# The first 40 microseconds of a decoder step: a weight copy moved to VectorE, the first matmuls sorted by kind, and the sums of squares in four wide batches

## The chip, the core and the metric

The kernel runs on one core of one Trainium2 chip. The metric is device microseconds from the start to the end of one execution. Three executions of the kernel before took 1449.05, 1449.08 and 1451.44 us, the median is 1449.08 us.

In what follows PE is TensorE (matmuls), PEld its weight loads, DVE is VectorE, ACT is ScalarE, POOL is GpSimd, and SP is the engine whose queue issues nearly all loads of weights.

## The reference

One inference step of a one-layer decoder, for a prompt of 256 tokens and 8 sample tokens, with a model width of 2048. All arithmetic is float32.

```python
xn = rmsnorm(x, g_mix)
z = xn @ w_in                                  # 2048 x 5128: inputs of two head groups
xr, conv_new = causal_conv(z[..., OFF_RGX:OFF_RGG], conv_buf, conv_w, conv_b)
...                                            # RG-LRU group and mLSTM group
x = x + jnp.concatenate([y_rg, y_ml], axis=-1) @ w_out
xq = (rmsnorm(x, g_xa) @ w_xa_q).reshape(B, L, XA_HEADS, XA_DH)
...                                            # attention over 256 memory tokens
x = x + o @ w_xa_o
xf = rmsnorm(x, g_ffn)
x = x + (jax.nn.silu(xf @ w_ffn_gate) * (xf @ w_ffn_up)) @ w_ffn_down
```

`rmsnorm` is `x * rsqrt(mean(x * x) + 1e-6) * g`. The change touches the first two lines alone: the norm of the input and the beginning of the product with `w_in`.

## The kernel before, in words

**Layout.** Activations stand with the features on the 128 partitions and the 264 tokens (256 + 8) along the free axis, as 16 chunks of 128 features each. `xres` holds the input that way. A product is a sequence of steps (the list `steps`). Most steps make 128 output features from all 16 input chunks and accumulate in one PSUM bank.

**Splitting.** A float32 product is made from parts in the type fp32r. Each operand is split in a high part and a low part: ACT copies the operand to fp32r (high), and DVE subtracts that copy from the operand (low). `mm3` then issues three matmuls: high weights times high input, high weights times low input, low weights times high input. In the words below these are hh, hl and lh. The weights of a step come in two halves of 1024 columns (512 KB each, tile `raw`, five buffers). ACT and DVE write the high and the low part of a half in one tile `w` (four buffers). A buffer of `raw` is free for SP's next load when both have read it.

**The norm comes late.** The factor `rsqrt(mean(x*x))` depends on the token alone, so products use the input times the gain (`g_mix`), and the results are multiplied by the factor when they leave PSUM. The sum of squares over features is built in `acc_x` (128 x 264): ACT squares, DVE adds. Matmuls with a vector of ones (`token_sums`) then add over partitions, DVE takes the inverse square root, and `spread` puts it back along the tokens in `rstd`.

**The first four steps** are special. They make four output blocks at once, in four PSUM banks `first`, and take four input chunks per step, so that PE can begin when a sixteenth of the input and of these weights has landed. One such sixteenth is called a chunk here, 0 to 15: an input piece (132 KB) and a weight piece (128 x 512, 256 KB), of which `split_first` makes high and low parts, and 12 matmuls (four banks times hh, hl, lh). Steps 4 to 6 are ordinary steps; step 7 has the gates.

**What sets the order.** Code is written as one program; a scheduler may reorder instructions of PE, DVE and ACT within their dependences, except inside a manual schedule, where the written order holds. SP's order is always as written. In the kernel before, PE's order is manual from step 4 to step 6 only. The squares are in two parts: eight of 128 x 264 after the splits of step 2 (seven of them with an addition on DVE), and two of 128 x 1056 with four additions after the splits of step 4. In step 5, before its chunk 9, PE issues `token_sums` of `acc_x`; in step 6, before its chunk 8, it issues `spread`. Both places are fixed in the program.

**Warm-up.** Before data has landed, PE runs eight float32 matmuls on a tile of ones that DVE sets.

Of the kernel before, what the change touches and what calls it, by code (L numbers as in the profile page):

```python
# [10 lines left out]
F32 = mybir.dt.float32  # L11
F32R = mybir.dt.float32r
I32 = mybir.dt.int32
AF = mybir.ActivationFunctionType
# [3 lines left out]
P = 128  # L18
# [4 lines left out]
N = T + NS  # L23
# [72 lines left out]
def layer_kernel(ctx: ExitStack, tc, xT, memT, vec, wrg, w_in, w_out, w_q, w_k, w_v, w_o,  # L96
                 w_gu, w_d0, w_d1, w_d2, c0T, kcT, vcT,
                 o_y, o_h, o_cp, o_cs, o_pc, o_sc, o_sn, o_m, o_k, o_v):
    nc = tc.nc
    act, dve, pe = Engine(nc.scalar, price_act), Engine(nc.vector, price_dve), Engine(nc.tensor, price_pe)  # L100
# [8 lines left out]
    def in_order():  # L109
        return tc.manual_schedule(engines={mybir.EngineType.Activation, mybir.EngineType.DVE})  # L110
# [4 lines left out]
    def nm(s):  # L115
        uid[0] += 1
        return f"{s}_{uid[0]}"

    def B(shape, dt=F32):
        return sb.tile(shape, dt, tag="B", bufs=NB, name=nm("B"))  # L120
# [12 lines left out]
    BW = 4 * N + 32  # L133
# [83 lines left out]
    def split_first(i, h):  # L217

        wh, wl = wrows(sb.tile([P, WW], F32R, tag="w", bufs=4, name=nm("w")), i)
        r = raws[i][h].rearrange("p (c m) -> p c m", m=P)  # L220
        with tc.high_priority(), in_order():
            for c in range(2):
                x, k = 4 * i + 2 * h + c, slice(4 * c, 4 * c + 4)
                split(*xn(x), xres[:, x, :], V("g_mix", x))
                st["split"] = act.activation(wh[:, k], r[:, k], AF.Copy)
                dve.tensor_sub(wl[:, k], r[:, k], wh[:, k].bitcast(F32))
        splits[i, h] = (wh, wl)

    def last_squares():

        a, b = (B([P, BW])[:, 0: 4 * N] for _ in range(2))
        for t, q in ((a, 2), (b, 3)):
            act.activation(t, xres[:, 4 * q: 4 * q + 4, :].rearrange("p c n -> p (c n)"), AF.Square)
        dve.tensor_add(a, a, b)
        dve.tensor_add(a[:, 0: 2 * N], a[:, 0: 2 * N], a[:, 2 * N:])
        dve.tensor_add(a[:, 0: N], a[:, 0: N], a[:, N: 2 * N])
        dve.tensor_add(acc_x, acc_x, a[:, 0: N])

    def wrows(w, i):

        w = w[:, WO: WO + 8 * N].rearrange("p (c n) -> p c n", n=N)
        return w[:, :, 0: P], w[:, :, P: 2 * P]
# [14 lines left out]
    def by2(x):  # L257

        return x.rearrange("p (a b) -> p a b", b=2)

    def turn(x):

        return x.rearrange("p (b a) -> p a b", b=2)
# [9 lines left out]
    def mm3(ps, a, b, start, stop):  # L273
        ah, al = a
        bh, bl = b
        ps, bh, bl = by2(ps), turn(bh), turn(bl)
        pe.matmul(ps, ah, bh, start=start, stop=False)
        pe.matmul(ps, ah, bl, start=False, stop=False)
        pe.matmul(ps, al, bh, start=False, stop=stop)

    st = {}
# [49 lines left out]
    ones = const.tile([P, P], F32, name="ones")  # L331
# [6 lines left out]
    def warm(n, w=None):  # L338

        ps = bank()  # L340
        for _ in range(n):
            pe.matmul(ps[:, :P], ones if w is None else w.to_broadcast([P, P]), ones, start=True, stop=True)

    warm(8)
    onesr = const.tile([P, P], F32R, name="onesr")
    mask = const.tile([P, P], F32, name="mask")
    pool_e.affine_select(out=mask, in_=ones, pattern=[[1, P]], compare_op=OP.is_ge, fill=0.0,
# [3 lines left out]
    def V(name, j=0, w=1):  # L351
        o = _V[name][0] + j
        return vecs[:, o: o + w]
# [67 lines left out]
    def sumsq(acc, x, first):  # L421
        if first:
            return act.activation(acc, x, AF.Square)
        s = tmp(x.shape[-1])
        i = act.activation(s, x, AF.Square)
        dve.tensor_add(acc, acc, s)
        return i

    def split(h, l, x, g):

        act.activation(h, x, AF.Copy, scale=g)
        dve.scalar_tensor_tensor(l, x, g, h.bitcast(F32), op0=OP.mult, op1=OP.subtract)
# [27 lines left out]
    xres = const.tile([P, KC, N], F32, name="xres")  # L460
    acc_x = const.tile([P, N], F32, name="acc_x")
# [531 lines left out]
    rx = lambda c: st["xn"](c)  # L993

    first = [bank("ax"), bank("ax"), bank("ax"), bank()]

    def pe_first(q):
        def f(i):
            w = W(i)
            for c in range(4):  # L1000
                for n in range(4):
                    mm3(first[n][:, :N], w(4 * c + n), rx(4 * q + c), q + c == 0, q + c == 6)
        return f

    def evac_first(_):
# [35 lines left out]
    def norm_x():  # L1041
        yield from rstd_from(acc_x, rstd, D)
# [388 lines left out]
    def load_x(e, lo, hi):  # L1431
        e.dma_start(xres[:, lo:hi, :], xT[:, lo:hi, :])
# [24 lines left out]
    for i, (src, cols, pef, evf, need) in enumerate(steps):  # L1457
        if i > 1:
            load_piece(i + LD - 1)
        if i == 7:  # L1460
            st["rg"] = side(rg_gen(), 0)
        if "pend" in need:
            with tc.high_priority(300):
                for e, x in pend:
                    e(x)
            pend = []
        for q in need:
            if q in st:
                finish(lambda: st[q].done)
        if not 4 <= i < 7:  # L1470
            with tc.high_priority(300):
                for e, x in pend:
                    e(x)
            pend = []
        if i == len(steps) - 1:
            kept.enter_context(tc.manual_schedule(engines={mybir.EngineType.PE}))
        now = pe.clock
        dve.clock, act.clock = max(dve.clock, now), max(act.clock, now)
        split_half(i + LS, 0)
        if i + LS < len(steps) and steps[i + LS][1] > 1024:  # L1480
            split_half(i + LS, 1)
        if i == 4:
            kept.enter_context(tc.manual_schedule(engines={mybir.EngineType.PE}))
        ps = pef(i)
        if i == 6:
            kept.close()
        if i == 1:
            with tc.issue_after(st["split"].ins):
                for c in range(8):
                    sumsq(acc_x, xres[:, c, :], c == 0)  # L1490
        if i == 3:
            with tc.issue_after(st["split"].ins), tc.high_priority():
                last_squares()
            st["rstd_x"] = Gen(norm_x())
        if evf is not None:
            pend.append((evf, ps))
        if i == 0:
            for c in range(0, 4, 2):
                load_x(sp, 12 + c, 14 + c)
                load_first(3, c)  # L1500
                load_first(3, c + 1)
        else:
            load_piece(i + LD)
        pump(pe.clock + SLACK)
        if i == 24:
            st["ng"] = side(ml_norm(), 6)
        if i == 57:
            PACE["full"] = False
        if i == 44:
            pool_e.dma_start(kept_k, ml["kb"])  # L1510
            for q in range(2):
                pool_e.dma_start(kept_v[q], ml["vts"][q])
        if i == 40:
            st["memg"] = side(mem_gen(), 7)
# [3 lines left out]
    for lo, hi in ((0, 1), (1, 2), (2, 4), (4, 6), (6, 8), (8, 10), (10, 12), (12, 14), (14, 16)):  # L1518
        for c in range(lo, hi):
            e, r = (pool_e, rstd) if c in POOLC else (dve, fin["ps"][:, :N])  # L1520
# [111 lines left out]
```

## Time and profile before

| | |
|---|---|
| median of three executions | 1449.08 us |
| the profiled execution | 1449.35 us |
| its span (first to last instruction) | 1447.4 us |
| PE busy | 1432.6 us, 99% of the span |
| DVE busy | 1046.6 us, 72% |
| ACT busy | 793.9 us, 55% |
| idle time of PE that a wait explains, over the span | 7.4 us in 12 waits |

The profile's page gives busy times and groups; the timeline gives the instructions in order, each row with its start, its length, the engine, the line, the operation, the tiles and, in brackets, the idle time of the engine before it with what ended it. Nearly all instructions carry the line of a recording helper (L61), so tiles are what tells them apart: `w<-raw` is the splitting of weights, `B<-xres,vecs` the splitting of the input, `t<-xres`, `acc_x` and `B<-xres` belong to the squares, `mm` and `ax` are PSUM banks. Matmuls are pipelined: a row's length includes the drain, so the pace is read from starts.

### The profile page before, as it was taken

The page shows a single profiled execution, that of the slowest core. Times are in us where ns is not written, and L with a number is a line of the kernel's source. Part 1 is how long each engine was busy: PE and PEld are TensorE (multiplying, and loading weights), DVE is VectorE, ACT ScalarE, POOL GpSimd, SP SyncE. Part 2 cuts the span into 40 slices and gives each one's busy share as a digit, 9 for nine tenths or more (in the row PEclk, how much of TensorE's full clock was granted, in tenths as well). Part 3 has the DMA queues.
Part 4 walks back from the last instruction along what each step waited for, and adds up shares of the span by engine and source line. Part 5 has one row for each costly group of instructions (what it writes and reads, how often), then busy time and mean ns, then how long its engine had stood idle before and what let it go on. Part 6 is the DMA issues. An engine that isn't in the chain of part 4 may idle for free.

```text
span 1447.4 us, 29983 instructions
## 1 busy us (share of the span) xinstructions
PE 1432.6 (99%) x11987; PEld 1407.3 (97%) x11987; DVE 1046.6 (72%) x2007; ACT 793.9 (55%) x1286; POOL 127.8 (9%) x203
## 2 busy tenths in 40 slices
PE   9999999999999999999999999999999999999997
PEld 9999999999999999899999999999999999999997
DVE  7966798998899999977676665555656655556564
ACT  7678785765556666655544444434444443444463
POOL 0001220000225433300000000000000000000000
PEclk9999999999999999999999999999999999999999
DMA  9645897548799887856555555555555555555573
GB/s 288 235 174 184 295 372 272 179 173 276 277 336 376 322 306 258 340 172 216 193 196 196 192 201 192 197 196 192 200 192 195 199 192 198 193 193 200 164 240 126
DMA packets 100764, 329.17 MB, mean 227 GB/s; under 512 B 11056, under 2 KB 19936, under 8 KB 100624
## 3 DMA queue, kind: packets, MB, share of 16 engines
q1 hardware_dynamic: 84336, 271.95, 54.1%
q0 software_dynamic: 15424, 54.22, 10.1%
q8 instruction: 93, 1.52, 0.4%
q10 hardware_dynamic: 864, 1.09, 0.2%
q14 instruction: 47, 0.39, 0.1%
HBM read 314.36 MB, written 12.86 MB: 226 GB/s over the span
## 4 chain that ended last, share of the span: by engine, by line
PE 56%; DVE 1%; issue 1%; DMA 0%; POOL 0%; ACT 0%; DVEq 0%; POOLq 0%; ACTq 0%
PE mm L61 56%; PE ax L61 1%; DVE B L61 1%; DVE dw L61 0%; DMA o_v<-B 0%; POOL ds L1182 0%; DVE w L61 0%; ACT B L61 0%; DVE c L61 0%; ACT dw L61 0%; DVE t L61 0%; ACT ds L61 0%; DVEq L1609 0%; ACT c L61 0%; DVEq L61 0%
## 5 line engine op out<-in xcount | busy, mean ns | idle before, releaser
L61 PE MATMUL mm<-B,w 128*128 128x264 f32 (+1 forms) x10960 | 1282.2, 279 | 1.8 <-DVE w L61 1.7
L61 PEld LDWEIGHTS mm<-B,w 128*128 128x128 f32 x10960 | 1261.5, 189 | 9.9 <-DVE w L61 2.3
L61 DVE TENSOR_TENSOR w<-raw,w 128x1024 fp32r<-128x1024 f32 (+1 forms) x522 | 624.4, 1198 | 303.5 <-ACT w L61 302.7
L61 ACT ACTIVATE w<-raw 128x1024 fp32r<-128x1024 f32 (+1 forms) x522 | 534.9, 1028 | 512.2 <-PE mm L61 347.8
L61 PE MATMUL mm<-w,B 128*128 128x512 f32 x384 | 86.9, 380 | 0.1
L61 PEld LDWEIGHTS mm<-w,B 128*128 128x128 f32 x384 | 70.6, 189 | 9.8 <-DVE w L61 0.5
L1521 POOL TENSOR_TENSOR B<-B,rstd 128x264 f32<-128x264 f32 x4 | 2.8, 738 | 802.9 <-ACT rstd L61 802.9
L61 DVE TENSOR_TENSOR t<-mm,rstd 128x264 f32<-128x264 f32 x96 | 41.4, 432 | 28.4 <-PE mm L61 28.3
L61 DVE SCALAR_TENSOR_TENSOR B<-B,dw 128x256 f32<-128x256 f32 x128 | 55.0, 483 | 3.2 <-ACT dw L61 3.0
L61 DVE TENSOR_TENSOR xres<-xres,mm 128x264 f32<-128x264 f32 (+1 forms) x81 | 34.3, 425 | 27.0 <-PE mm L61 27.0
L61 DVE SCALAR_TENSOR_TENSOR dw<-B,qsm,dw 128x256 f32<-128x256 f32 x96 | 48.6, 511 | 2.6 <-ACT dw L61 1.8
L61 PE MATMUL ax<-B,B 128*128 128x256 f32 (+3 forms) x272 | 44.9, 305 | 1.1 <-DVE B L61 1.0
L1182 POOL TENSOR_TENSOR ds<-dw,ds 128x256 fp32r<-128x256 f32 x32 | 35.4, 1106 | 106.8 <-ACT ds L61 106.7
L61 PEld LDWEIGHTS ax<-B,B 128*128 128x128 f32 x272 | 37.9, 191 | 3.8 <-DVE B L61 1.6
L61 ACT ACTIVATE B<-xres,vecs 128x264 fp32r<-128x264 f32 (+1 forms) x64 | 32.2, 503 | 4.2 <-DVE xres L61 2.7
L61 ACT ACTIVATE dw<-B,qsm 128x256 f32<-128x256 f32 x32 | 16.2, 508 | 27.0 <-issue 13.9
L1171 POOL DMA_DIRECT2D B<-kcT x32 | 17.3, 541 | 139.6 <-DVE B L61 126.5
L61 ACT ACTIVATE t<-xres 128x264 f32<-128x264 f32 (+1 forms) x53 | 21.1, 409 | 15.3 <-DVE xres L61 15.2
L61 ACT ACTIVATE dw<-B,B 128x128 f32<-128x128 f32 x64 | 21.2, 393 | 11.2 <-DMA B<-scr 7.9
L61 DVE SCALAR_TENSOR_TENSOR B<-xres,vecs,B 128x264 fp32r<-128x264 f32 x48 | 23.4, 490 | 4.1 <-ACT B L61 4.1
L61 ACT ACTIVATE dw<-ax,dw 128x256 f32<-128x256 f32 x32 | 15.1, 471 | 19.3 <-DVE dw L61 18.3
L61 ACT ACTIVATE B<-t 128x264 fp32r<-128x264 f32 (+1 forms) x60 | 24.1, 409 | 2.1 <-DVE t L61 2.1
(176 smaller groups left out, 679.0 us busy)
## 6 DMA issues: line engine op xcount, KB each, us to landing
raw<-w_gu SPq DMA_DIRECT2D x176, 512.0 KB, 3.6
raw<-w_d SPq DMA_DIRECT2D x80, 512.0 KB, 3.6
raw<-w_in SPq DMA_DIRECT2D x74, 512.0 KB, 5.2
raw<-w_out SPq DMA_DIRECT2D x32, 512.0 KB, 3.7
raw<-w_q SPq DMA_DIRECT2D x32, 512.0 KB, 6.2
B<-kcT POOLq DMA_DIRECT2D x32, 512.0 KB, 8.8
B<-vcT POOLq DMA_DIRECT2D x32, 512.0 KB, 9.9
raw<-w_k SPq DMA_DIRECT2D x32, 512.0 KB, 5.0
```

Source lines behind the costliest of these rows:

```text
L61: return f(*a, **k)
L1171: pool_e.dma_start(kc, kcT[h, b])
L1182: pool_e.tensor_sub(ws[:, 1], acc, ws[:, 0].bitcast(F32))
L1521: e.tensor_mul(st["y"](c), st["y"](c), r)
```

## The change

Five things are different.

1. The high part of chunk 0's weights is made by DVE (`tensor_copy`, before it does anything else for that chunk) and no longer by ACT.
2. In chunk 0 the 12 matmuls are written as four hh, four hl, four lh.
3. PE's manual schedule begins with step 0, where it began with step 4. In chunks 1 to 15 the order is now the written one of `mm3`.
4. All 16 chunks' squares are made in four wide batches of 128 x 1056 on ACT, with two or three additions on DVE for each: batches 0 and 1 after the splits of step 4, batches 2 and 3 after the splits of step 5. The eight narrow squares after step 2's splits are gone.
5. The warm-up has nine matmuls, on a constant that exists before the kernel's own first instruction, with no tile of ones to wait for.

```diff
             for c in range(2):
                 x, k = 4 * i + 2 * h + c, slice(4 * c, 4 * c + 4)
+                if x == 0:
+                    dve.tensor_copy(wh[:, k], r[:, k])
                 split(*xn(x), xres[:, x, :], V("g_mix", x))
-                st["split"] = act.activation(wh[:, k], r[:, k], AF.Copy)
+                if x > 0:
+                    st["split"] = act.activation(wh[:, k], r[:, k], AF.Copy)
                 dve.tensor_sub(wl[:, k], r[:, k], wh[:, k].bitcast(F32))
...
-    def last_squares():
-
-        a, b = (B([P, BW])[:, 0: 4 * N] for _ in range(2))
-        for t, q in ((a, 2), (b, 3)):
-            act.activation(t, xres[:, 4 * q: 4 * q + 4, :].rearrange("p c n -> p (c n)"), AF.Square)
-        dve.tensor_add(a, a, b)
-        dve.tensor_add(a[:, 0: 2 * N], a[:, 0: 2 * N], a[:, 2 * N:])
-        dve.tensor_add(a[:, 0: N], a[:, 0: N], a[:, N: 2 * N])
-        dve.tensor_add(acc_x, acc_x, a[:, 0: N])
+    def squares(q):
+
+        t = B([P, BW])[:, 0: 4 * N]
+        act.activation(t, xres[:, 4 * q: 4 * q + 4, :].rearrange("p c n -> p (c n)"), AF.Square)
+        dve.tensor_add(t[:, 0: 2 * N], t[:, 0: 2 * N], t[:, 2 * N:])
+        if q == 0:
+            dve.tensor_add(acc_x, t[:, 0: N], t[:, N: 2 * N])
+            return
+        dve.tensor_add(t[:, 0: N], t[:, 0: N], t[:, N: 2 * N])
+        dve.tensor_add(acc_x, acc_x, t[:, 0: N])
...
-            pe.matmul(ps[:, :P], ones if w is None else w.to_broadcast([P, P]), ones, start=True, stop=True)
-
-    warm(8)
+            pe.matmul(ps[:, :P], w, w, start=True, stop=True)
+
+    warm(9, nc.const_aps.tensor(1.0, [P, P], F32))
...
             for c in range(4):
+                if q + c == 0:
+                    for k, l in ((0, 0), (0, 1), (1, 0)):
+                        for n in range(4):
+                            pe.matmul(by2(first[n][:, :N]), w(n)[k], turn(rx(0)[l]), start=k + l == 0, stop=False)
+                    continue
                 for n in range(4):
-                    mm3(first[n][:, :N], w(4 * c + n), rx(4 * q + c), q + c == 0, q + c == 6)
+                    mm3(first[n][:, :N], w(4 * c + n), rx(4 * q + c), False, q + c == 6)
...
-        if i == 4:
+        if i == 0:
             kept.enter_context(tc.manual_schedule(engines={mybir.EngineType.PE}))
         ps = pef(i)
         if i == 6:
             kept.close()
-        if i == 1:
-            with tc.issue_after(st["split"].ins):
-                for c in range(8):
-                    sumsq(acc_x, xres[:, c, :], c == 0)
-        if i == 3:
+        if i in (3, 4):
             with tc.issue_after(st["split"].ins), tc.high_priority():
-                last_squares()
-            st["rstd_x"] = Gen(norm_x())
+                for q in range(2):
+                    squares(2 * i - 6 + q)
+            if i == 4:
+                st["rstd_x"] = Gen(norm_x())
```

The splits of step i + 1 are issued while step i is written, so what stands under `i in (3, 4)` comes behind the splits of steps 4 and 5 (the fifth and sixth step).

**ACT, from chunk 11 to chunk 12.** Before: `w_269` is the weights of chunks 10 and 11, `B_258` the input of chunks 8 to 11, `t_330` and so on the narrow squares, `B_358` and `w_355` the input and weights of chunk 12 and on.

```order
L61 ACTIVATE B_258<-xres,vecs 128x264
L61 ACTIVATE w_269<-raw_138 128x4x128
L61 ACTIVATE acc_x<-xres 128x264
L61 ACTIVATE t_330<-xres 128x264
L61 ACTIVATE t_333<-xres 128x264
L61 ACTIVATE t_336<-xres 128x264
L61 ACTIVATE t_339<-xres 128x264
L61 ACTIVATE t_342<-xres 128x264
L61 ACTIVATE t_345<-xres 128x264
L61 ACTIVATE B_358<-xres,vecs 128x264
L61 ACTIVATE w_355<-raw_248 128x4x128
```

Now, with `w_272` for chunks 10 and 11 and `B_339`, `w_336` for chunk 12 and on, `w_350` for chunks 14 and 15, and `w_414` for the first half of step 4:

```order
L61 ACTIVATE B_261<-xres,vecs 128x264
L61 ACTIVATE w_272<-raw_139 128x4x128
L61 ACTIVATE B_339<-xres,vecs 128x264
L61 ACTIVATE w_336<-raw_251 128x4x128
...
L61 ACTIVATE w_350<-raw_255 128x4x128
L61 ACTIVATE w_414<-raw_332 128x8x128
L61 ACTIVATE w_417<-raw_334 128x8x128
L61 ACTIVATE B_468<-xres 128x1056
L61 ACTIVATE B_472<-xres 128x1056
```

Seven squares stood between chunk 11's and chunk 12's splits, and now none does. The first squares come behind both halves of step 4.

**DVE, from the splits of step 4 to the sums' reader.** Before: `w_433` and `w_436` are the halves of step 4, `w_499` and `w_502` of step 5, `w_560` and `w_563` of step 6; `c_598` is what DVE reads of PE's `token_sums`.

```order
L61 TENSOR_TENSOR w_433<-raw_351,w_433 128x8x128
L61 TENSOR_TENSOR w_436<-raw_353,w_436 128x8x128
L61 TENSOR_TENSOR B_487<-B_487,B_488 128x1056
L61 TENSOR_TENSOR B_487<-B_487 128x528
L61 TENSOR_TENSOR w_499<-raw_429,w_499 128x8x128
L61 TENSOR_TENSOR B_487<-B_487 128x264
L61 TENSOR_TENSOR w_502<-raw_431,w_502 128x8x128
L61 TENSOR_TENSOR acc_x<-acc_x,B_487 128x264
L61 TENSOR_TENSOR w_560<-raw_495,w_560 128x8x128
L61 TENSOR_TENSOR w_563<-raw_497,w_563 128x8x128
L61 TENSOR_SCALAR c_598<-ax_594 128x3
```

Now, from the first half of step 5 on (`w_481`, `w_484`; step 6 is `w_550`, `w_553`). Ahead of these rows stand both halves of step 4, the 528-wide additions of batches 0 and 1 and batch 0's addition that sets `acc_x`.

```order
L61 TENSOR_TENSOR w_481<-raw_410,w_481 128x8x128
L61 TENSOR_TENSOR B_472<-B_472 128x264
L61 TENSOR_TENSOR w_484<-raw_412,w_484 128x8x128
L61 TENSOR_TENSOR acc_x<-acc_x,B_472 128x264
L61 TENSOR_TENSOR B_536<-B_536 128x528
L61 TENSOR_TENSOR B_541<-B_541 128x528
L61 TENSOR_TENSOR B_536<-B_536 128x264
L61 TENSOR_TENSOR B_541<-B_541 128x264
L61 TENSOR_TENSOR w_550<-raw_477,w_550 128x8x128
L61 TENSOR_TENSOR acc_x<-acc_x,B_536 128x264
L61 TENSOR_TENSOR w_553<-raw_479,w_553 128x8x128
L61 TENSOR_TENSOR acc_x<-acc_x,B_541 128x264
```

The last addition to `acc_x` stood behind four of these half splits (steps 4 and 5). It now stands behind six (steps 4, 5 and 6).

**PE, in chunk 1.** `B_149` is the high part and `B_150` the low part of the input, `w_146` holds both parts of the weights; a row with the high input that comes behind a row with the low input, of the same bank, is lh. Before:

```order
L61 MATMUL ax_109<-B_149,w_146 128x264
L61 MATMUL ax_110<-B_149,w_146 128x264
L61 MATMUL ax_111<-B_149,w_146 128x264
L61 MATMUL mm_112<-B_149,w_146 128x264
L61 MATMUL ax_109<-B_150,w_146 128x264
L61 MATMUL ax_110<-B_150,w_146 128x264
L61 MATMUL ax_111<-B_150,w_146 128x264
L61 MATMUL mm_112<-B_150,w_146 128x264
L61 MATMUL ax_109<-B_149,w_146 128x264
```

Now (`B_151`, `B_152` and `w_147` in the same roles):

```order
L61 MATMUL ax_110<-B_151,w_147 128x264
L61 MATMUL ax_110<-B_152,w_147 128x264
L61 MATMUL ax_110<-B_151,w_147 128x264
L61 MATMUL ax_111<-B_151,w_147 128x264
L61 MATMUL ax_111<-B_152,w_147 128x264
L61 MATMUL ax_111<-B_151,w_147 128x264
```

The first matmul that needs the low part of the chunk's weights was the ninth of the chunk, and is now the third. `token_sums` of `acc_x` stand at the same place of PE's order as before: in step 5, behind eight chunks of its first half and one of its second.

## The prediction

> **What bounds the kernel now.** I read the page first, then PE's waits, then the timeline of the stretch that the change touches. On the page:
>
> ```profile
> span 1447.4 us, 29983 instructions
> PE 1432.6 (99%) x11987; PEld 1407.3 (97%) x11987; DVE 1046.6 (72%) x2007; ACT 793.9 (55%) x1286; POOL 127.8 (9%) x203
> ```
>
> PE is busy for all but 14.8 us of the span. None of the edits shortens PE's own work, so they can only add or remove idle time of PE. PE's waits (engine, tile, what it waited for: us in total, times, longest):
>
> ```profile
> PE ax L61 <- DVE B L61: 2.0, 3, 1.0
> PE mm L61 <- DVE w L61: 1.7, 2, 1.5
> PE ax L61 <- ACT w L61: 1.5, 2, 1.1
> PE mm L61 <- DVE ones L61: 1.1, 1, 1.1
> ```
>
> The last two rows lie in the first 25 us and are what the change can take away, 2.6 us at most; the first two come later. The timeline from the start to chunk 1 (start, length, instruction, idle time before it):
>
> ```profile
> 0.81 0.66 SPq L214 DMA_DIRECT2D raw<-w_in  x1
> ...
> 1.12 3.78 PE L61 MATMUL mm<-ones 128*128 128x128 f32 x16 [1.12 <-DVE ones L61]
> ...
> 4.22 0.51 ACT L61 ACTIVATE B<-xres,vecs 128x264 fp32r<-128x264 f32 x1 [1.01 <-DMA vecs<-vec]
> 4.64 0.61 ACT L61 ACTIVATE w<-raw 128x512 fp32r<-128x512 f32 x1
> ...
> 5.30 1.68 PE L61 MATMUL ax<-B,w 128*128 128x264 f32 x6 [0.39 <-ACT w L61]
> ...
> 6.89 0.63 ACT L61 ACTIVATE w<-raw 128x512 fp32r<-128x512 f32 x1 [1.24 <-DMA raw<-w_in]
> ...
> 7.56 0.69 DVE L61 TENSOR_TENSOR w<-raw,w 128x512 fp32r<-128x512 f32 x1 [1.18 <-ACT w L61]
> ...
> 7.58 0.61 PE L61 MATMUL ax<-B,w 128*128 128x264 f32 x3
> ...
> 9.12 0.94 PE L61 MATMUL ax<-B,w 128*128 128x264 f32 x6
> ```
>
> (Between those rows of PE lie the rest of chunk 0 and chunk 1.) Chunk 0 begins at 5.30 because ACT's copy of the weights ends at 5.25. Chunk 1 begins at 7.58, and what ends last there is a landing: its weights arrive at about 6.88, ACT copies them until 7.53. The same chain binds at chunk 10, and another wait stands at chunk 12:
>
> ```profile
> 19.43 0.63 ACT L61 ACTIVATE w<-raw 128x512 fp32r<-128x512 f32 x1 [0.87 <-DMA raw<-w_in]
> ...
> 20.10 0.69 DVE L61 TENSOR_TENSOR w<-raw,w 128x512 fp32r<-128x512 f32 x1 [0.87 <-ACT w L61]
> 20.12 0.94 PE L61 MATMUL ax<-B,w 128*128 128x264 f32 x6
> ...
> 21.21 1.97 ACT L61 ACTIVATE t<-xres 128x264 f32<-128x264 f32 x6
> ...
> 22.81 0.28 PE L61 MATMUL mm<-B,w 128*128 128x264 f32 x1
> ...
> 23.50 0.62 ACT L61 ACTIVATE w<-raw 128x512 fp32r<-128x512 f32 x1
> 24.16 0.60 PE L61 MATMUL ax<-B,w 128*128 128x264 f32 x3 [1.08 <-ACT w L61]
> ```
>
> What a matmul of 264 columns takes when nothing is late is read from the chain of waits, whose longest unbroken piece but one is
>
> ```profile
> 645.25 80.33 PE mm L61 x714
> ```
>
> 0.1125 us from start to start, 1.35 for the 12 matmuls of a chunk. So PE could have begun chunk 12 at 22.92 and began at 24.16: ACT had squares in front of that chunk's splits. Chunk 2 began at 9.12; eight chunks on is 19.92, and chunk 10 began at 20.12: PE goes at the pace at which pieces land, with 0.2 us to spare.
>
> **The change part by part.** *Copy on DVE, chunk 0 by kind, warm-up.* The first weights, issued at 0.81, land 3.5 us later, at 4.3. The trace has no wide DVE copy; its price lies between half the width here
>
> ```profile
> raw<-w_in SPq DMA_DIRECT2D x1, 256.0 KB, 3.5
> ...
> L61 DVE TENSOR_SCALAR B<-B,B 128x256 f32<-128x256 f32 x8 | 2.2, 350 | 0.0
> ```
>
> (0.35 us; the row above it is the landing) and the subtraction of the full width, 0.69; I take 0.5, since a copy reads one operand as the row does. It ends between 4.7 and 5.0, at my value at 4.85. ACT's part of the input ends at 4.73. The warm-up has 18 records where 16 took 3.78; at 0.22 each it is 0.45 longer, and if it starts at 0.82, when SP's first issue shows the engines are let go, PE is free at 4.85, its last record's drain aside, and at 5.15 if it still starts at 1.12. So chunk 0 begins at about 4.9, 0.4 earlier. PE is slow there (6 matmuls in 1.68, about 0.25 each, until 6.9 or so), which takes its 12 to between 7.3 and 7.9. This gains nothing: chunk 1's weights still land at 6.88, ACT's copy of them is where it was, PE waits until 7.58. Without that cover the three edits together would be worth 0.4 us.
>
> *The order of chunks 1 to 15.* The third matmul of a chunk, 0.23 us after its first, now needs DVE's low part, which ends 0.69 us after DVE takes over from ACT. Where a chunk waits for its landing this is a new wait. Chunk 1: low part at 8.25, PE goes on at 8.30, 0.50 late; chunk 2 is then reached at 9.42 in place of 9.12 and waits 0.2 again, for its low part at 9.8, and ends at 10.96. Chunks 3 to 9 at 1.35 each take PE to 20.41. There the high part is ready (20.12) and the low part comes at 20.79, so the third matmul waits 0.2. Chunk 10 ends at 21.96, chunk 11 at 23.31. Before, the end of chunk 11 was 22.92: this part costs 0.4 us.
>
> *No squares before chunk 12.* Its weights, issued at
>
> ```profile
> 15.75 0.54 SPq L214 DMA_DIRECT2D raw<-w_in  x1
> ...
> raw<-w_in SPq DMA_DIRECT2D x1, 256.0 KB, 5.9
> ```
>
> and 5.9 us on the way, land at 21.7; ACT copies until 22.4, DVE's low part is ready at 23.1. PE at 23.31 waits for nothing: 0.85 us earlier than 24.16. Later pieces land one after another ahead of PE's need.
>
> *Squares behind steps 4 and 5.* This is the term that decides. The rows that price it:
>
> ```profile
> 20.01 1.48 SPq L177 DMA_DIRECT2D raw<-w_in  x2
> ...
> 29.10 2.05 ACT L61 ACTIVATE B<-xres 128x1056 f32<-128x1056 f32 x2
> ...
> 32.48 0.71 DVE L61 TENSOR_TENSOR B<-B 128x528 f32<-128x528 f32 x1
> 33.10 1.22 DVE L61 TENSOR_TENSOR w<-raw,w 128x1024 fp32r<-128x1024 f32 x1
> 34.24 0.43 DVE L61 TENSOR_TENSOR B<-B 128x264 f32<-128x264 f32 x1
> 34.58 1.22 DVE L61 TENSOR_TENSOR w<-raw,w 128x1024 fp32r<-128x1024 f32 x1
> 35.72 0.43 DVE L61 TENSOR_TENSOR acc_x<-acc_x,B 128x264 f32<-128x264 f32 x1
> ...
> 38.31 0.72 PE L61 MATMUL ax<-ones,acc_x 128*128 128x1 f32 x6
> ```
>
> ```profile
> raw<-w_in SPq DMA_DIRECT2D x1, 512.0 KB, 6.3
> ```
>
> Before, `acc_x` was complete at 36.15 and PE's `token_sums` came at 38.31, 2.2 us later. Now PE comes earlier: from chunk 12 it has 123 matmuls to go, 4 chunks and step 4 of 48 each and 27 of step 5; at 0.1125 that is 13.84 us, so it is there at 37.15. (Before it took 14.15, with three short waits in it that fall.) And `acc_x` comes later. From start to start a DVE split takes 33.10 to 34.24, 1.14 us; a 264-wide addition 0.34; a 528-wide one 0.62. Step 4's first half lands at 20.01 + 6.3 = 26.3; ACT's copy, priced like a square of nearly the same width (the two in 2.05 are 0.98 apart and 1.07 long), ends at 27.45. From there DVE has no break until the sums are done: six half splits 6.84, four 528-wide additions 2.48, seven 264-wide ones 2.38, together 11.70; one addition that waits for its predecessor's result 0.12, two waits of 0.1 for ACT, and 0.09 for the last one's drain. 27.48 + 12.1 = 39.6. ACT is not the limit: step 4's second half is copied by 28.65, two squares end at 30.7, step 5's copies at 32.6, two squares at 34.6, seven small ones and step 6's copies at 37.2, each ahead of DVE's need by 0.1 us or more. So PE waits at `token_sums` from 37.15 to 39.6, 2.45 us. Queued behind them on PE are the rest of step 5 and all that follows. DVE and ACT go on with step 7's splits, the buffers of `raw` that step 5 and 6 free come free before the wait ends, and SP's queue has the same order, so nothing more is late.
>
> *Sum.* Before, PE was at `token_sums` at 38.31; now at 39.6. From there the order on all engines is the same but for a few neighbours, and what stands behind moves with PE. +1.3 us on the profiled execution of 1449.35 us, which is 0.27 above the median; on the median, 1449.08 + 1.3 = **1450.4 us**. The bounds of this term: DVE's chain could lose ACT's waits and begin at once (39.3) or meet 0.6 more of them (40.2), +1.0 to +1.9.
>
> **The rivals.** *The stall does not come* (DVE clears the chain by 37.15). Then the gains stand alone: 37.15 - 38.31 = -1.16, 1447.9 us. For it: DVE's work before step 4 falls too. Against it: the chain begins with a landing, 26.3, which no edit moves, and needs 12 us of DVE for which 9.7 are there.
>
> *Later waits take the delay up.* The first two rows of PE's waits, 3.7 us, come later. The longest of them:
>
> ```profile
> 195.00:209.00 14.00, 12.24 (x102) 11.53 (x101) 14.00 (x49) 11.54 (x27) 1.06 (x2) 1.00 1.00 377
> ...
> 208.61 1.62 PE L61 MATMUL mm<-B,w 128*128 128x264 f32 x12 [1.54 <-DVE w L61]
> ```
>
> DVE is busy for all 14 of those 14 us and the DMA engines' share is 1.00. If their pace does not hang on PE, a PE that comes 1.3 late waits 1.3 less: 1449.1 us. Against it: the work that fills DVE there is started by PE's own results, so it is late by the same.
>
> *The clock falls during the stall* (the slower side). At the end of the execution the granted clock halves after PE's last matmul:
>
> ```profile
> 1439.25 1.03 PE L61 MATMUL ax<-B,B 128*128 128x258 f32 x4
> ...
> 1443.80:1447.40 3.60, 0.00 (x0) 0.00 (x0) 0.00 (x0) 0.00 (x0) 0.00 (x0) 0.51 0.53 201
> ```
>
> The seventh figure behind the length, PEclk, is 0.51 from 1443.8 on, 3.5 us after PE went idle; the idle time of 1.54 at 208.61 left it at 1.00. A wait of 2.45 us lies between. If it is enough, matmuls go at 0.22 in place of 0.11 us until the clock is back; at the start PE ran slow from 1.12 to about 6.9, 5.8 us, so the loss is up to half of that, 2.9: 1453.3 us. The point from which it decides is the idle time at which the clock falls, somewhere between 1.5 and 3.5. [...]
>
> *The start counts after all* (the landings move with it): another 0.4 on top of the missing stall, 1447.5. Chunk 10's wait speaks against it.
>
> **How the numbers follow.** Forecast 0.56; later waits take it up 0.17; no stall 0.12; clock falls 0.06; the start counts 0.02; something not seen 0.07, as likely fast as slow. About 0.2%, 2.9 us, is what a measurement can tell from no change: 1446.2 to 1452.0. The forecast and three of the rivals lie inside; beyond it on the slow side are the fallen clock and half of what I have not seen, 0.10; on the fast side the other half, 0.04; within, 0.86. The forecast's own range is 1449.7 to 1451.3; with no stall at the low end and a third execution of 1451.44 before, I take 1447.7 to 1452.2.
>
> **What would show it.** PE's `token_sums` row at about 39.6 with 2 us or more of idle time, ended by DVE `acc_x`, would show the deciding step right; a start at 37 would show it wrong. The chunk-12 wait gone, and PE at chunk 12 at 23.3; `ax` waits for DVE `w` in chunks 1, 2 and 10 in place of those for ACT; chunk 0's first matmul at 4.9 but chunk 1's still at 7.58. DVE's last addition to `acc_x` ending at 39.5 and beginning right behind a split of step 6. The wait at 208 at 1.5 says that the delay was carried through, at 0.2 that it was taken up. A PEclk below 1.00 between 39 and 46 would show the fallen clock. The prediction is wrong if chunk 12 still waits or if the median is below 1449 or above 1451.5.

## The result, and the profile after

The changed kernel is slower, by 0.16%, which is little but clear of the noise: 1452.23 us (median of 22 executions, 1450.12 to 1455.80) against 1449.98 us (22 executions, 1448.57 to 1451.77) of the kernel before. The ratio is 1.0016, with a 95% interval of 1.0010 to 1.0023: +2.25 us where +1.3 was forecast. The larger sample also put the kernel before 0.9 us higher than the three executions from which the forecast started. So of the miss of 1.83 us (1452.23 - 1450.4) about half is the base, 0.9, and half the change itself, 0.95. The ratio, here and below, is the one on record with its interval; it is not the quotient of the two medians beside it and can lie 0.0006 from it.

The profiled execution of the changed kernel took 1452.66 us. PE's waits, in the columns known from before (what was waited for: us in total, times, longest):

```profile
PE ax L61 <- DVE acc_x L61: 2.4, 1, 2.4
PE ax L61 <- DVE B L61: 2.0, 3, 1.0
PE mm L61 <- DVE w L61: 1.7, 2, 1.5
PE ax L61 <- ACT B L61: 1.1, 2, 0.7
PE mm L61 <- PEq L1611: 0.8, 1, 0.8
PE ax L61 <- DVE w L61: 0.6, 3, 0.2
PE ax L61 <- ACT w L61: 0.4, 1, 0.4
```

The row for the tile of ones is gone, the one for ACT's `w` has shrunk from 1.5 to 0.4, and a row that was not there stands on top: 2.4 us for `acc_x`. (The row of 0.8 is the time before the warm-up, which now starts at 0.85.) The timeline shows the start and chunk 1 as forecast (chunk 0 at 4.83 where 4.9 was said; the copy on DVE took 0.43):

```profile
4.19 0.43 DVE L61 CAST w<-raw 128x512 fp32r<-128x512 f32 x1 [3.12 <-DMA raw<-w_in]
...
4.83 0.60 PE L61 MATMUL ax<-B,w 128*128 128x264 f32 x3 [0.35 <-ACT B L61]
...
6.10 0.63 ACT L61 ACTIVATE w<-raw 128x512 fp32r<-128x512 f32 x1 [0.80 <-DMA raw<-w_in]
...
6.78 0.30 PEld L61 LDWEIGHTS ax<-B,w 128*128 128x128 f32 x2 [0.30 <-ACT w L61]
6.78 0.49 PE L61 MATMUL ax<-B,w 128*128 128x264 f32 x2
...
7.51 1.05 PE L61 MATMUL ax<-B,w 128*128 128x264 f32 x7 [0.23 <-DVE w L61]
```

Chunk 1 (its weight load, in the row of PEld) waits first for ACT's copy, which waits for the landing, and after two matmuls again for DVE's low part. Its landing came 0.8 us earlier in this execution than in the profiled one of before; so much do landings differ. Further on, PE's rows:

```profile
20.73 0.49 PE L61 MATMUL ax<-B,w 128*128 128x264 f32 x2 [0.39 <-ACT w L61]
21.45 1.05 PE L61 MATMUL ax<-B,w 128*128 128x264 f32 x7 [0.23 <-DVE w L61]
...
24.03 1.18 PE L61 MATMUL ax<-B,w 128*128 128x264 f32 x9
```

Chunk 10 waits for its landing and its low part, chunk 12 begins at 24.03 without a wait, where it began at 24.16 with one of 1.08. Then comes the place that decided, on DVE and on PE:

```profile
27.84 1.23 DVE L61 TENSOR_TENSOR w<-raw,w 128x1024 fp32r<-128x1024 f32 x1 [0.71 <-ACT w L61]
29.54 1.23 DVE L61 TENSOR_TENSOR w<-raw,w 128x1024 fp32r<-128x1024 f32 x1 [0.48 <-ACT w L61]
...
38.81 1.21 DVE L61 TENSOR_TENSOR w<-raw,w 128x1024 fp32r<-128x1024 f32 x1
39.94 0.42 DVE L61 TENSOR_TENSOR acc_x<-acc_x,B 128x264 f32<-128x264 f32 x1
```

```profile
36.30 1.74 PE L61 MATMUL mm<-B,w 128*128 128x264 f32 x14
40.42 0.83 PE L61 MATMUL ax<-ones,acc_x 128*128 128x1 f32 x6 [2.38 <-DVE acc_x L61]
41.11 5.06 PE L61 MATMUL mm<-B,w 128*128 128x264 f32 x28
```

From 27.84 to 40.36 DVE has one break, 0.48 us for the late second half of step 4. PE idles 2.38 us, and after that its 28 recorded matmuls take 5.06 us, 0.18 each where 0.11 is the pace. The windows (length, busy time of PE, PEld, DVE, ACT and POOL with counts, then the granted clock PEclk, the DMA share and GB/s) say why:

```profile
34.48:37.89 3.41, 3.41 (x32) 3.36 (x30) 3.41 (x7) 3.41 (x10) 0.00 (x0) 1.00 0.73 244
37.89:41.30 3.41, 1.02 (x9) 0.88 (x8) 3.41 (x5) 1.04 (x2) 0.00 (x0) 1.00 0.69 229
41.30:44.71 3.41, 3.41 (x17) 3.41 (x17) 2.67 (x23) 0.00 (x0) 0.00 (x0) 0.50 0.87 267
44.71:48.12 3.41, 3.41 (x32) 3.41 (x32) 1.53 (x4) 1.06 (x1) 0.00 (x0) 1.00 0.16 62
```

From 41.30 to 44.71 the granted clock is 0.50, for one stretch of 3.41 us, and PE gets 17 matmuls through it where 32 fit: about 1.7 us lost. That is the rival to which the prediction gave a chance of 0.06. The rest is carried through: the wait near 208 of before comes at 213.48, as long as it was. Of the 4.9 us by which it is later, 2.1 are the later `token_sums` (40.42 for 38.31), 1.7 the half clock, and 0.74 a wait at 181.9 that the trace of before has not. At the last matmul 3.5 us are left. The wait at 181.9 does not come with the squares: it is 0.94 in the run with the start of the change alone, and the runs with the sums late and with the stall filled have none.

```profile
213.48 1.73 PE L61 MATMUL mm<-B,w 128*128 128x264 f32 x13 [1.53 <-DVE w L61]
```

### The profile page after: what moved, and what is told of

Same layout as the page of the kernel before. It is cut to its first block, busy times and chain, and to the rows that moved or that the text cites. A ratio compares the mean times of both kernels' runs of the same rounds, so it can differ in the third digit from the quotient of the medians.

```text
span 1451.0 us, 29978 instructions
## 1 busy us (share of the span) xinstructions
PE 1433.9 (99%) x11989; PEld 1408.5 (97%) x11989; DVE 1045.8 (72%) x2008; ACT 793.4 (55%) x1279; POOL 128.5 (9%) x203
## 4 chain that ended last, share of the span: by engine, by line
PE 56%; DVE 1%; issue 1%; POOL 0%; ACT 0%; DVEq 0%; DMA 0%; POOLq 0%; ACTq 0%
PE mm L61 56%; PE ax L61 1%; DVE B L61 1%; DVE dw L61 0%; POOL ds L1191 0%; DVE w L61 0%; POOL B L1245 0%; ACT B L61 0%; DVE c L61 0%; POOL o_v L1289 0%; ACT dw L61 0%; DVE t L61 0%; ACT ds L61 0%; DMA o_k<-t 0%; DVEq L1616 0%
```

## The experiments

The theory after these two traces: the change costs a stall at `token_sums` that PE carries to the end, and on top of it a stretch of half clock that this stall sets off in most executions. The rivals: A, the written order of the matmuls in chunks 1 to 15 costs it; B, the stall alone costs it, and the half clock comes of something else; C, something behind the norm costs it. Every comparison is between 11 executions of the version and 27 or 33 of the kernel before on the same chip. "Mean clock" below is the mean granted clock of an execution, to three digits.

### token_sums later

```diff
-                if (i, c) in ((5, 9), (6, 8)):
+                if (i, c) in ((6, 1), (6, 12)):
```

> The changed kernel with token_sums put behind the first chunk of the next projection step (its spread behind the thirteenth), so that TensorE meets it some 8 us later. The theory (the stall at token_sums, 2.4 us in the profiled run of the change, and the stretch of half clock that it sets off, 1.65 us there) expects no wait for acc_x, no half clock near 41 us, and 1452.66 - 2.4 - 1.65 = 1448.6 us, about 1.4 below the kernel before. Rival A (the written order of the matmuls of chunks 1 to 15 costs it) expects the time to stay at the change's 1452.2. Rival B (the stall alone; the half clock has another cause) expects 1452.2 - 2.4 = 1449.8, with the half clock still there in some executions. Rival C (something behind the norm, such as the new wait at 182 us) expects no more than the stall's part to go and the later waits to stay: 1450 to 1452.

1449.52 us against 1450.46, ratio 0.9994 (0.9985 to 1.0002). The row for `acc_x` is gone from PE's waits, and the clock stays whole. PE's timeline:

```profile
35.76 4.89 PE L61 MATMUL mm<-B,w 128*128 128x264 f32 x42
40.48 0.72 PE L61 MATMUL ax<-ones,acc_x 128*128 128x1 f32 x6
41.07 3.96 PE L61 MATMUL mm<-B,w 128*128 128x264 f32 x33
45.57 0.68 PE L61 MATMUL ax<-ident,c 128*128 128x128 f32 x4 [0.54 <-DVE c L61]
```

`token_sums` runs at the same time as in the changed kernel, 40.5, but PE has work until then. Rival A falls, since the written order is all there. C falls too: nothing behind the norm was touched. The gain against the kernel before, 0.9 us by the medians, is smaller than the 1.4 expected, and its interval reaches over 1; the last row can be a part of that, since PE now waits 0.54 for the result of `token_sums` before `spread`.

### The stall filled

Eleven matmuls on a constant fill the time in which PE waits; the sum on DVE, and so the delay, stay.

```diff
-    warm(9, nc.const_aps.tensor(1.0, [P, P], F32))
+    fin["one"] = nc.const_aps.tensor(1.0, [P, P], F32)
+    warm(9, fin["one"])
...
+                if (i, c) == (5, 9):
+                    fill = bank("ax")
+                    for _ in range(11):
+                        pe.matmul(fill[:, :P], fin["one"], fin["one"], start=True, stop=True)
                 if (i, c) in ((5, 9), (6, 8)):
```

> The changed kernel with eleven matmuls on a constant (fp32, 128x128, what they write is not used) just ahead of token_sums, so that TensorE is busy where it waited. The delay of token_sums stays, its idle time is filled. The theory expects token_sums still near 40.4 us, no half clock behind it, and 1452.66 - 1.65 = 1451.0 us with a narrow spread of executions. Rival B (the half clock does not come from the idle time) expects the change's 1452.2 and its wide spread, 1450 to 1456. Rival A expects 1452.2.

1451.05 us against 1450.46, ratio 1.0003 (0.9994 to 1.0011). The executions lie within 1.9 us (1450.29 to 1452.17); those of the changed kernel within 5.7 (22 executions) and 4.4 (11). `token_sums` comes at 39.88, right behind the filling, in which each matmul shows as two records:

```profile
37.20 2.62 PE L61 MATMUL ax<-const-float32-1.0 128*128 128x128 f32 x22
39.88 0.83 PE L61 MATMUL ax<-ones,acc_x 128*128 128x1 f32 x6
```

Two windows of its trace:

```profile
37.36:40.77 3.41, 3.35 (x31) 3.16 (x30) 3.41 (x6) 0.86 (x1) 0.00 (x0) 1.00 0.66 217
40.77:44.19 3.42, 3.42 (x32) 3.42 (x32) 2.87 (x25) 0.98 (x1) 0.00 (x0) 1.00 0.81 280
```

No half clock, 32 matmuls in the second. So the delay alone is worth about 0.6 us by the medians, and with it alone the change could not be told from none. Rival B falls: with the idle time the half clock goes, and with it about 1.7 us of the 2.25 (2.25 - 0.59, from two comparisons).

### The squares as before

The changed kernel with the old squares: eight narrow ones behind the splits of step 2 (the code's step one), the rest in two wide batches behind those of step 4.

```diff
-    def squares(q):
+    def last_squares():
...
-        if i in (3, 4):
+        if i == 1:
+            with tc.issue_after(st["split"].ins):
+                for c in range(8):
+                    sumsq(acc_x, xres[:, c, :], c == 0)
+        if i == 3:
             with tc.issue_after(st["split"].ins), tc.high_priority():
-                for q in range(2):
-                    squares(2 * i - 6 + q)
-            if i == 4:
-                st["rstd_x"] = Gen(norm_x())
+                last_squares()
+            st["rstd_x"] = Gen(norm_x())
```

(The body of `last_squares` is that of the kernel before.)

> The changed kernel with the input's squares as they were before: eight on their own behind the splits of step one, the rest in two wide batches behind step three. First piece on VectorE, first chunk by kind, shorter warm-up and the written order of chunks 1 to 15 stay. The theory expects the wait of 0.9 us at chunk 12 back, token_sums near 38.3 us as before, no half clock, and no difference from the kernel before: 1449.6 to 1450.2 us. Rival A (the written order) expects it to stay near 1452.

1449.73 us against 1450.46, ratio 0.9997 (0.9988 to 1.0006): no difference, as expected, and the squares are the part of the change that costs. Its trace has the wait at chunk 12 back, now in two parts, and `token_sums` near its old place:

```profile
24.00 0.49 PE L61 MATMUL ax<-B,w 128*128 128x264 f32 x2 [0.58 <-ACT w L61]
24.99 1.05 PE L61 MATMUL ax<-B,w 128*128 128x264 f32 x7 [0.50 <-DVE w L61]
...
38.71 0.72 PE L61 MATMUL ax<-ones,acc_x 128*128 128x1 f32 x6
```

### token_sums later, and chunks 1 to 15 in the scheduler's order

```diff
-                if (i, c) in ((5, 9), (6, 8)):
+                if (i, c) in ((6, 1), (6, 12)):
...
-        if i == 0:
+        if i == 4:
             kept.enter_context(tc.manual_schedule(engines={mybir.EngineType.PE}))
```

> The changed kernel with token_sums put later as in the other run, and TensorE's order of chunks 1 to 15 left to the scheduler, as before the change. The theory expects the time of the run with token_sums late less the waits for the low parts that the written order adds, 0.4 us at most by the row of waits: 1448.2 to 1448.6 us. Rival A expects this run, and not the one with token_sums late alone, to fall below the kernel before.

1449.09 us against 1450.46, ratio 0.9992 (0.9983 to 1.0001); 1448.2 to 1448.6 was expected. It was compared once more on another chip:

> The kernel with token_sums late and the scheduler's order in chunks 1 to 15 again, since its first comparison (0.9992, 0.9983 to 1.0001) left open whether it is faster than the kernel before. The theory expects 1.0 to 1.4 us below the kernel before (0.9990 to 0.9993).

1449.47 us against 1450.42, ratio 0.9993 (0.9984 to 1.0002). Each interval reaches just over 1. The two are independent; their mean is 0.99925, and with intervals of equal width the interval of the mean is narrower by the root of two, 0.0009 / 1.41 = 0.0006: 0.9986 to 0.9999. That version is thus probably faster than both kernels, by about 1 us of 1450. Whether the scheduler's order has a part in it cannot be told: the version with the written order gave 0.9994.

### The changed kernel again, beside three others

> The changed kernel itself, so that the others of this comparison stand beside it on the same chip. Both theories expect what was measured for it: about 2.2 us above the kernel before (1.0016), with some executions 3 to 5 us above it.

1452.33 us against 1450.08, ratio 1.0015 (1.0005 to 1.0024): the result repeats. Its trace has the stall (2.14 us) and the half clock, from 41.47 to 44.88.

### Half of the stall filled

As the run with the stall filled, with five matmuls in place of eleven.

```diff
-                    for _ in range(11):
+                    for _ in range(5):
```

> As the run with eleven matmuls on a constant ahead of token_sums, but with five: 5 x 0.223 = 1.1 us of the 2.4 us are filled, 1.3 us stay idle, and token_sums comes when it came. The theory expects that the half clock needs more idle time than this in a stretch of 3.41 us, as waits of 1.3 to 1.5 us elsewhere leave the clock whole in the profiles of both kernels: the time of the run with eleven, 1451.1 us, and few executions with a mean clock below 0.998. If the half clock comes of any idle time above about 1 us, the time is that of the changed kernel, 1452.2 to 1452.7 us. If the idle time were not the cause, also that.

1451.37 us against 1450.08, ratio 1.0003 (0.9994 to 1.0012). The time is between that of the changed kernel and that of the run with eleven, and one of the 11 executions had a mean clock below 0.998 (5 of 11 of the changed kernel beside it). But that one is the profiled execution, and its trace contradicts what was expected of 1.3 us of idle time:

```profile
36.97 1.28 PE L61 MATMUL ax<-const-float32-1.0 128*128 128x128 f32 x10
39.63 0.80 PE L61 MATMUL ax<-ones,acc_x 128*128 128x1 f32 x6 [1.38 <-DVE acc_x L61]
40.29 5.96 PE L61 MATMUL mm<-B,w 128*128 128x264 f32 x36
...
212.34 3.87 PE L61 MATMUL mm<-B,w 128*128 128x264 f32 x32 [1.53 <-DVE w L61]
```

```profile
37.07:40.48 3.41, 2.03 (x18) 1.87 (x17) 3.41 (x5) 0.97 (x2) 0.00 (x0) 1.00 0.67 228
40.48:43.89 3.41, 3.41 (x17) 3.41 (x17) 2.93 (x25) 0.00 (x0) 0.00 (x0) 0.50 0.85 267
```

1.38 us of idle time here, and the clock fell; 1.53 us near 212 in the same execution, and it did not. The changes of the clock within one execution lie a multiple of 3.413 us apart: in the trace of the changed kernel at 3.75, 41.30, 44.71 and 1447.59, which is steps of 11, 1 and 411 times 3.4133 us, and in that of before at 6.84 and 1443.85, 421 times. That gives each trace a grid of stretches, and a boundary of this one's, at 211.15, divides the wait of 1.53 us. So this pair alone does not tell what sets the two apart. Two other stretches tell more. In the run with `token_sums` later, a wait of 1.54 us lies whole in one stretch:

```profile
207.04:210.45 3.41, 1.87 (x15) 1.64 (x14) 3.41 (x14) 3.41 (x8) 0.00 (x0) 1.00 0.86 344
210.45:213.86 3.41, 3.41 (x33) 3.41 (x32) 3.41 (x9) 2.53 (x4) 2.12 (x4) 1.00 0.95 320
```

In the changed kernel run again, the stretch with most of the stall:

```profile
38.05:41.47 3.42, 2.08 (x18) 2.08 (x19) 3.32 (x11) 0.00 (x0) 0.00 (x0) 1.00 0.81 240
41.47:44.88 3.41, 3.41 (x18) 3.41 (x18) 1.58 (x16) 1.06 (x1) 0.00 (x0) 0.50 0.76 240
```

With 1.87 us of busy time the clock held, and with 2.08 us it fell. So neither the length of the idle time nor PE's busy time by the profile sets these two apart. What differs is that six of the 18 matmuls in the second stretch are those of `token_sums`, of a single column each. I then counted, in every stretch of the grid, the time that matmuls of 128 columns and more fill, each at its pace from start to start: 0.11 us in most rows, 0.22 in those of 512 columns (0.216 is the median in the trace of before) and of 258 (the four at 1439.25 there start at 1439.25, 1439.47, 1439.69 and 1439.91). Of the ten traces that there were, four had a fall before the last matmul, behind shares of 0.03, 0.14, 0.33 and 0.38. All other stretches between the first release and the one with the last matmul had 0.43 or more, and left the clock whole.

### Filled with matmuls of one column

This tests that reading. The only difference from the run with eleven matmuls is the number of columns.

```diff
-                        pe.matmul(fill[:, :P], fin["one"], fin["one"], start=True, stop=True)
+                        pe.matmul(fill[:, :1], fin["one"], fin["one"][:, 0:1], start=True, stop=True)
```

> As the run with eleven matmuls on a constant ahead of token_sums, but each over one column in place of 128: the same number of issues at the same pitch of 0.112 us, so TensorE is as busy by the profile, and token_sums comes at the same time; what they write is not used. In ten profiles so far the clock halved behind those windows of 3.413 us in which matmuls of 128 columns and more filled under about 0.38 of the time, and no one-column matmul of token_sums counted. If that is the rule, these one-column matmuls count as idle: a window near 38 to 41 us is empty as in the change, half clock in about two executions of three, and the time is that of the changed kernel, 1452.2 to 1452.9 us, 1.2 to 1.8 above the run with 128 columns beside it. If the clock goes by whether TensorE is busy by the profile, no half clock, and the time of the run with 128 columns, 1451.1 us.

> The run with eleven matmuls over 128 columns again, so that it stands beside the one-column run on the same chip. Both theories expect 0.6 to 1.3 us above the kernel before, no half clock and few executions with a mean clock under 0.999.

With one column 1452.46 us against 1450.42, ratio 1.0012 (1.0003 to 1.0022). With 128 columns, on the same chip, 1451.09, ratio 1.0000 (0.9992 to 1.0009). The means of the two lie 1.6 us apart, 0.5 to 2.7 by twice their standard error. PE's timeline and windows with one column:

```profile
37.39 2.51 PE L61 MATMUL ax<-const-float32-1.0 128*128 128x1 f32 x22
40.06 0.90 PE L61 MATMUL ax<-ones,acc_x 128*128 128x1 f32 x6 [0.16 <-DVE acc_x L61]
```

```profile
37.20:40.61 3.41, 3.25 (x32) 3.20 (x30) 3.41 (x5) 1.27 (x2) 0.00 (x0) 1.00 0.73 234
40.61:44.02 3.41, 3.41 (x17) 3.41 (x17) 3.21 (x25) 0.00 (x0) 0.00 (x0) 0.50 0.88 312
```

By the profile PE is busy for 3.25 of the 3.41 us, 0.16 us of idle time is left, and the clock halves all the same. With 3.35 busy us of 128 columns (the run above) it stays. The two programs differ in nothing but the columns: in these two traces the filling of 128 columns was followed by a clock of 1.00, and that of one column by 0.50. In the three traces of this comparison the count has one more fall, behind 0.06 in the first of these stretches, and no other stretch under 0.41.

### The order of chunks 1 to 15 alone undone

The changed kernel with PE's manual schedule from step 4 on, as before.

```diff
-        if i == 0:
+        if i == 4:
             kept.enter_context(tc.manual_schedule(engines={mybir.EngineType.PE}))
```

> The changed kernel with TensorE's order of chunks 1 to 15 left to the scheduler, as before the change; token_sums stays where the change has it. The theory expects no gain: TensorE comes to token_sums up to 0.4 us earlier and waits as much longer there, since the sum on VectorE ends when it ended; half clock as in the change: 1452.2 to 1452.7 us. Rival A (the written order costs it) expects it to fall to the kernel before, 1450.0 to 1450.5 us.

1452.86 us against 1450.08, ratio 1.0017 (1.0008 to 1.0026). Rival A falls for the second time. No execution has a mean clock above 0.998, and the trace has the stall and the half clock as in the changed kernel:

```profile
40.26 0.83 PE L61 MATMUL ax<-ones,acc_x 128*128 128x1 f32 x6 [2.40 <-DVE acc_x L61]
```

### The start of the change alone

The edit of the old squares above, and with it:

```diff
-        if i == 0:
+        if i == 4:
             kept.enter_context(tc.manual_schedule(engines={mybir.EngineType.PE}))
```

> Of the change only its start: first piece on VectorE, the first chunk's matmuls by kind, nine matmuls of warm-up, with the input's squares and the order of chunks 1 to 15 as before the change. The theory expects no difference from the kernel before (0.2 us either way): the second chunk's weights bind. The rival that the start counts expects 0.4 to 0.9 us below the kernel before.

1449.39 us against 1450.08, ratio 0.9995 (0.9986 to 1.0004). No difference can be told. With the run of the old squares (0.9997) it leans to a gain of about 0.6 us, worked out like the mean above as 0.9996 with 0.9990 to 1.0002, so that stays open. The traces cannot settle it either: chunk 1 began between 6.78 and 7.84 us in the twelve traces that have the new start, by its landing, and at 7.58 in the one of before.

## Why the prediction was wrong

**Chunk 0, the copy and the warm-up** were as the prediction had them: chunk 0 begins 0.47 us earlier (4.83 for 5.30), the copy costs 0.43 where 0.5 was taken, and chunk 1 is bound by its landing. That it gains nothing at the end is neither contradicted nor shown.

**The order of chunks 1 to 15.** The waits came where they were expected: 0.23 us behind chunk 1's second matmul (0.50 was said) and 0.23 in chunk 10 (0.2); the one said for chunk 2 came in chunk 4 (0.17). Undone, the time did not fall (1.0017 beside 1.0015): the order lies ahead of a stall that takes such waits up.

**No squares before chunk 12.** The wait of 1.08 us is gone, as the prediction said. PE reached chunk 12 at 24.03 and not at 23.31, as chunk 10's weights came 0.6 us later in this execution; six other traces with this order and no squares there have 22.74 to 23.95.

**The squares behind steps 4 and 5**, the deciding step, held in kind and size: DVE's chain runs from the landing of step 4's first half without a break but one, ends at 40.36 (39.6 was said; its start was 0.36 later, and the break is 0.48), and PE waits 2.38 us (2.45 was said).

**The delay carried to the end.** The wait near 208 is 1.53 us after and 1.54 before, so the rival that later waits take the delay up falls. So does the rival without a stall. The size may have been high: with the half clock kept away, the whole change cost 1.0003 and 1.0000 (the two filled runs), 0.6 to 0.7 us by the medians. +1.3 is just inside the first interval and at the end of the second, so it is not refuted. In the traces `token_sums` came between 1.1 and 2.1 us later than in the one trace of before (39.39 to 40.42 for 38.31), and one trace for before cannot say which is typical.

**The clock is the step that failed.** The prediction named the fall of the clock and the slower side, and gave it 0.06, since it looked for an idle time at which the clock falls, "somewhere between 1.5 and 3.5". What the runs showed in its place: of the stretches of 3.413 us between the first release and the one with the last matmul, the five that matmuls of 128 columns and more filled to 0.38 or less were followed by a fall, and those filled to 0.41 or more were not. The 3.5 us at the end of the trace of before, from which the upper end of that range came, hold one whole stretch without a matmul, from 1440.44 to 1443.85, and the fall at its end: an empty stretch was enough there, which does not show that it is needed. A share of 0.38 was followed by a fall too, and in the changed kernel 2.4 us of stall with 0.67 us of one-column matmuls behind it are 3.1 us without wide matmuls.

How often the clock falls can be estimated from these numbers, if the share is taken as what decides. A share of 0.38 leaves 0.62 x 3.41 = 2.1 us empty. If a boundary of the grid splits the gap into x and 3.1 - x, the clock would fall for x over 2.1 or under 1.0, which is 2.0 of 3.1 positions, and always where no boundary is in the gap: by this estimate two executions in three together. The mean clocks agree with that but are too coarse to test it, as they also hold the half clock behind the last matmul, whose length differs (3.51 us in the trace of before, 3.37 in that of the changed kernel). The five traces with a fall have 0.997 or 0.998, the eight without 0.998 or 0.999. Of the 33 executions of the changed kernel 12 have 0.997 or less, 15 have 0.998 and 6 have 0.999, so by these traces between 12 and 27 fell. Of the 22 with the fill of 128 columns none has less than 0.998 and 20 have 0.999; of the 93 of the kernel before beside the experiments, two have 0.997 and none less. The six of the changed kernel with 0.999 took 1450.12 to 1451.18 us, and the 12 with 0.997 or less 1452.40 to 1455.80. Three of these have 0.996 (1454.23, 1454.83 and 1455.80 us). By an estimate that is 10 us or more at half clock (twice 0.0035 of 1453 us), where the most in any trace is 8.2 (3.4 behind the stall and 4.8 at the end), so they probably had a second stretch; no trace shows one.

Its price was lower than the prediction's "up to" 2.9 us, which came from the slow start of the trace of before: the half clock in the four traces of the first ten lasted 3.41 us, and 17 or 18 matmuls went through where 32 fit, 1.6 to 1.7 us lost.

With 1.3 + 1.7 added to its base, the forecast would have been 1452.1, next to the 1452.23 measured. That nearness would have been partly luck, since the base was 0.9 low and not every execution has the fall. With the base of the larger sample, 1449.98, and +1.3 the forecast would have been 1451.3, still 0.95 short.

## What to carry to other kernels

A wait is priced by more than its length. In these traces, between the clock's first release and the stretch with the last matmul, every stretch of 3.41 us that wide matmuls filled to 0.38 or less was followed by one at half clock, which cost another 1.6 to 1.7 us, and that was so with one-column matmuls in the stall too (3.25 of 3.41 us busy by the profile). Put the reader of a late result behind work that does not need it: moving `token_sums` eight chunks on cost two numbers and was worth about 3 us against the changed kernel (1.0016 less 0.9994 of 1450; 2.7 by the medians of two comparisons). When a sum is moved to relieve one engine, follow the other engine's queue up to the reader, since the last addition stood behind the half splits of step 6 as well.

## What was not expected of the hardware

- With one-column matmuls in the stall TensorE was busy for 3.25 of 3.41 us by the profile, and the clock was 0.50 in the next window; with 128 columns it was busy for 3.35 us, and the clock stayed 1.00.
- Over all 13 traces the count of wide matmuls separates the stretches without an exception: five falls before the last matmul behind shares of 0.38 or less, and no fall behind 0.41 or more. The stretch that holds the last matmul in the run with the old squares had 0.39 and held. Between 0.38 and 0.41 there is this one stretch, so the border is an estimate. What the hardware counts is not shown.
- The grid's phase differs between executions: the clock was first released at between 3.75 us (the changed kernel) and 6.84 us (before) in the traces; in these two, PE's matmuls start 0.21 to 0.22 us apart up to there and 0.11 from there on. So, by the estimate above, the same stall would cost 1.7 us more in one execution than in the next. That would be a part of the spread of the changed kernel (standard deviation 1.5 us, and 0.5 and 0.9 in the two filled runs), but not all spread is that: the executions of the kernel before, 3.2 us apart in the first comparison, lay up to 6.4 apart in the later ones.
